# First loads in smaller parts, two fewer matmuls of ones, and the turned norms at another place in TensorE's order: a two-layer encoder trunk in fp32

## The chip, the cores and the metric

The kernel runs on one core of one Trainium2 chip. The metric is device time in microseconds (us) for one execution. The kernel before was run three times: median 651.51 us, lowest 651.26, highest 651.71.

## What is computed

The reference is a trunk of two layers over 512 tokens of width 1024. Layer 0 mixes tokens by neighbourhood attention, layer 1 by latent attention. After each layer a gated per-layer embedding is added. Only the start of the program matters for this change:

```python
xn = rmsnorm(x, norm_g[0])                      # x / sqrt(mean(x*x) + 1e-6) * g
q, k, v, z = split(xn @ w_in, 4)                # mixer_na
...
y = (o * silu(z)) @ w_out
h = x + y
gate = sigmoid(rmsnorm(h, ple_norm[0]) @ ple_w_gate[0])
x = h + gate * (p[0] @ ple_w_proj[0])
```

`p[0] @ ple_w_proj[0]` depends on no other result and can be computed first. `z` can be computed from x times its gains without the norm, and multiplied by each token's inverse norm afterwards.

## The kernel before

Every matrix product is done with fp32 values split in two parts: `hi` is a copy in the matmul's format, written by ScalarE, and `lo` is what is left, written by VectorE or GpSimd. A product of two split operands takes three matmuls: hi·hi, hi·lo and lo·hi. A matmul has 128 rows and 512 columns.

The start of `run` (from L1190) goes like this.

- `NWARM` = 11 matmuls of a constant of ones into a scratch PSUM tile open TensorE's work (L1192, L1193). Their result is not used.
- `ple_load` (L648) loads layer 0's p (`pT`) and its two weight tiles (`proj`), each 128x1024, in halves of 128x512 (256 KB). The halves of `pT` are issued by ScalarE's queue, the four of `proj` by SyncE's (L656). Each half is split by ScalarE (L658, `whi`) and VectorE (L659, `wlo`).
- SyncE then issues the gains, the eight tiles of x transposed (L1209), the weights of the first two z tiles in halves (L1216), the identity, and x with the third z tile's weights (L1224, L1225).
- `ple` computes p times the weights. Its first two output tiles, for tokens 0 to 127 and 128 to 255, are written in an order of their own (L677 to L679): for each of them first the three matmuls of the first half of the contraction, then those of the second half.
- `z_phase` with `ws` computes the first two z tiles (L201, 48 matmuls); without it the next three: z2 from weights already split, z3 and z4 from weights loaded by `load_w` (L99 the load, L100 `wwhi` on ScalarE, L101 `wwlo` on GpSimd).
- The inverse norms of the tokens (`ssq`) come from four sums of squares on ScalarE (L1226) and three short operations on GpSimd (L1228 to L1230). Four transposes of 128x128 on TensorE (L156, called by L1231) spread them over a PSUM tile, "the turns" below. ScalarE copies it to `R` (L1234). VectorE multiplies z0 and z1 by `R` (L193), and then x transposed by the turned tile and the gains (L1238); ScalarE and VectorE split that (L1239 `xh`, L1240 `xl`). The q and k products (L418) use it.

A tile scheduler sets the order of the instructions on each engine, except where `issue_after` or `InOrder` pins one behind another. Each engine works through its own instructions in that order. A DMA of SyncE or ScalarE is issued by a place in that engine's order. The buffers of `wraw`, `whi` and `wlo` are three each and are reused in turn.

Of the kernel before, what the change touches and what calls it, by code (L numbers as in the profile page):

```python
# [13 lines left out]
F32 = mybir.dt.float32  # L14
F32R = mybir.dt.float32r
AF = mybir.ActivationFunctionType
ALU = mybir.AluOpType
AX = mybir.AxisListType
PSUM = bass.MemoryType.PSUM
P = 128  # L20
S = 512
D = 1024
NT = S // P
KD = D // P
# [1 line left out]
EPS = 1e-6  # L26
NEG = -3.0e38
QSC = 96.0 ** -0.5
NWARM = 11
NLATE = 3  # L30
NEARLY = 7
SEVEN = (0, 1)
# [24 lines left out]
class Trunk:  # L57
# [123 lines left out]
    def z_phase(self, wap, xT, js, after=None, R=None, ws=None, first=None):  # L181


        zs = {}
        nc = self.nc

        def finish(j, ps):
            z = zs[j] = self.zp.tile([P, S], F32, name="z", tag="z")
            with self.tc.issue_after(after) if after is not None else nullcontext():
                if R is None:  # L190
                    nc.scalar.activation(z, ps, AF.Silu)
                else:
                    nc.vector.tensor_tensor(out=z, in0=ps, in1=R, op=ALU.mult)  # L193
                    nc.scalar.activation(z, z, AF.Silu)

        if ws:
            pss = [self.psum("mm") for j in js]
            for k in range(0, KD, 2):
                for ps, w in zip(pss, ws):
                    for i, (l, r) in enumerate(self.terms(w, xT, (k, k + 1))):  # L200
                        nc.tensor.matmul(ps, l, r, start=k == 0 and i == 0, stop=k == KD - 2 and i == 5)  # L201
            for j, ps in zip(js, pss):
                finish(j, ps)
            return zs
        for j in js:
            w = first if first and j == js[0] else self.load_w(wap[j], 1024)
            ps = self.psum("S" if R is not None and j < 4 else "mm")
            self.proj_T(ps, w, xT)
            finish(j, ps)
        return zs  # L210

# [433 lines left out]
    def ple_load(self, layer, pool=None):  # L645

        nc, a = self.nc, self.a
        if layer:  # L648
            return [self.load_w(ap, 1024) for ap in (a["pT"][1], a["proj"][1, 0], a["proj"][1, 1])]
        t = [[pool.tile([P, 1024], d, name=n, tag="p" + n, bufs=3) for n, d in (("wraw", F32), ("whi", F32R), ("wlo", F32R))]  # L650
             for _ in range(3)]
        src = (a["pT"][0], a["proj"][0, 0], a["proj"][0, 1])
        last = None
        for i, c0, c1 in [(i, c, c + S) for c in (0, S) for i in (1, 0)] + [(2, 0, S), (2, S, 2 * S)]:
            raw, hi, lo = (x[:, c0:c1] for x in t[i])
            (nc.sync if i else nc.scalar).dma_start(raw, src[i][:, c0:c1])  # L656
            with self.tc.issue_after(last.ins) if last else nullcontext():
                last = nc.scalar.activation(hi, raw, AF.Copy)  # L658
            nc.vector.tensor_tensor(out=lo, in0=raw, in1=hi.bitcast(F32), op=ALU.subtract)  # L659
        return [(hi, lo) for raw, hi, lo in t]  # L660

    def ple(self, pool, layer, tag, bufs, operands):
        nc, a = self.nc, self.a
        pT = operands[0]
        first = []
        for n in range(2):
            wj = operands[1 + n]
            for t in range(NT):
# [4 lines left out]
                if n == 0 and t < 2:  # L673
                    first.append((pp, m))
                    if t == 1:
                        last = None
                        for i in (0, 1, 2, 6, 7, 8, 3, 4, 5, 9, 10, 11):  # L677
                            with self.tc.issue_after(last.ins) if last else nullcontext():
                                last = nc.tensor.matmul(first[i // 6][0], *first[i // 6][1][i % 6], start=i % 6 == 0, stop=i % 6 == 5)  # L679
                else:  # L680
                    self.mms(pp, m)
                if n == 0 and t == 0:
# [494 lines left out]
    def run(self):  # L1177
        tc, nc, a = self.tc, self.nc, self.a
# [9 lines left out]
        with tc.tile_pool(name="pre", bufs=4, reuse_waits="tile") as pool:  # L1188
            R = pool.tile([P, S], F32, name="R", bufs=1)
            ones = [nc.const_aps.tensor(1.0, (P, n), mybir.dt.bfloat16) for n in (P, S)]  # L1190
            ps = self.psum("T")
# [3 lines left out]
            g0 = pool.tile([P, KD], F32, name="g0", bufs=1)  # L1195
            nc.sync.dma_start(g0, a["g0"])

            raw, xT = pair("r"), pair("x")
# [4 lines left out]
            xs = [xk[k // 4][:, k % 4, :] for k in range(KD)]  # L1203
# [24 lines left out]
            nc.gpsimd.tensor_scalar(ss, ss, 1.0 / D, EPS, op0=ALU.mult, op1=ALU.add)  # L1228
            nc.gpsimd.tensor_scalar(self.rows[0][0], ss, 1.0, None, op0=ALU.add)
            nc.gpsimd.tensor_tensor(out=ss, in0=ss, in1=self.half.to_broadcast([P, NT]), op=ALU.pow)  # L1230
            turned = self.transposes([ss[:, t:t + 1].to_broadcast([P, P]) for t in range(NT)])  # L1231
            nc.scalar.activation(first[1], first[0], AF.Copy)
            nc.gpsimd.tensor_tensor(out=first[2], in0=first[0], in1=first[1].bitcast(F32), op=ALU.subtract)
            nc.scalar.activation(R, turned, AF.Copy)  # L1234
            zs = self.z_phase(a["na_z"], raw, range(2), R=R, ws=ws)
            for k in range(KD):
                hi, lo = part(xT, k)
                nc.vector.scalar_tensor_tensor(xs[k], turned, g0[:, k:k + 1], xs[k], op0=ALU.mult, op1=ALU.mult)  # L1238
                nc.scalar.activation(hi, xs[k], AF.Copy)  # L1239
                nc.vector.tensor_tensor(out=lo, in0=xs[k], in1=hi.bitcast(F32), op=ALU.subtract)  # L1240
            zs.update(self.z_phase(a["na_z"], raw, range(2, 8 - NLATE), R=R, first=first[1:]))
# [239 lines left out]
```

## Time and profile before

| | |
|---|---|
| median of 3 runs | 651.51 us (651.26 to 651.71) |
| the profiled execution, its own time | 651.45 us |
| its span | 649.3 us (2.15 us lie around it) |
| TensorE busy | 639.7 us, 99% of the span |
| ScalarE, VectorE, GpSimd busy | 454.6, 429.6 and 407.3 us |

TensorE (PE in the rows) is busy nearly all the time, and the weight loads (PEld) run beside its matmuls. Three more views matter: which waits PE had, what stands at the start of the program in order of time, and what stands around the turns.

### The profile page before, as it was taken

What the parts mean: (1) busy time and instruction counts of PE and PEld (TensorE: products, weight loads), DVE (VectorE), ACT (ScalarE), POOL (GpSimd) and SP (SyncE); (2) the same over time, 40 slices, a digit from 0 to 9 for tenths busy, and PEclk for the clock granted to TensorE, in tenths of its full rate; (3) what the DMA queues carried; (4) which work ended last, traced back from release to release, by engine and by line L of the source; (5) the groups of instructions that cost most, each with busy time, mean ns of one, the idle gap of its engine ahead of it and who ended that gap; (6) DMA issues with size and microseconds to landing.
All of it is one profiled execution on the core that took longest, in us unless ns stands there. A gap on an engine that the chain in (4) does not pass through costs nothing.

```text
span 649.3 us, 9981 instructions
## 1 busy us (share of the span) xinstructions
PE 639.7 (99%) x3299; PEld 541.9 (83%) x3299; DVE 429.6 (66%) x887; ACT 454.6 (70%) x903; POOL 407.3 (63%) x370
## 2 busy tenths in 40 slices
PE   9999999999999999999999999999999999999994
PEld 6888888888888888888999888888888888888884
DVE  6197995665665626569715515888988885574665
ACT  7575776887887752797644536888989897547855
POOL 0371015777978673896655515786959887437974
PEclk9999999999999999999999999999999999999998
DMA  9939725878968988354642254120111222683514
GB/s 327 357 129 298 222 97 193 243 195 213 255 197 208 238 204 325 132 182 172 220 138 99 78 135 133 46 58 24 54 46 66 65 95 102 234 293 121 194 66 163
DMA packets 46131, 107.41 MB, mean 165 GB/s; under 512 B 4736, under 2 KB 17792, under 8 KB 46080
## 3 DMA queue, kind: packets, MB, share of 16 engines
q1 hardware_dynamic: 34608, 87.12, 39.1%
q0 software_dynamic: 11040, 18.88, 13.5%
q10 hardware_dynamic: 432, 0.79, 0.3%
q8 instruction: 26, 0.43, 0.3%
q14 instruction: 25, 0.20, 0.1%
HBM read 95.23 MB, written 25.17 MB: 185 GB/s over the span
## 4 chain that ended last, share of the span: by engine, by line
PE 98%; ACT 1%; DVE 0%; issue 0%; POOLq 0%; POOL 0%; DVEq 0%; ACTq 0%
PE ps_mm L124 28%; PE ps_S L124 12%; PE ps_mm L965 7%; PE ps_T L156 6%; PE ps_T L857 5%; PE ps_O L1077 5%; PE ps_mm L857 3%; PE ps_mm L418 3%; PE ps_T L302 3%; PE ps_S L857 3%; PE ps_T L124 3%; PE ps_O L124 2%; PE ps_O L613 2%; PE ps_mm L915 2%; PE ps_S L302 2%; PE ps_mm L201 2%
## 5 line engine op out<-in xcount | busy, mean ns | idle before, releaser
L101 POOL TENSOR_TENSOR wwlo<-wraw,wwhi 128x1024 fp32r<-128x1024 f32 (+5 forms) x68 | 121.1, 1795 | 96.5 <-ACT wwhi L100 45.6
L802 POOL TENSOR_TENSOR wlo<-wraw,whi 128x512 fp32r<-128x512 f32 x56 | 73.7, 1351 | 24.8 <-ACT whi L800 18.6
L1062 POOL TENSOR_TENSOR ex<-ex,rc 128x512 f32<-128x512 f32 x64 | 66.3, 1045 | 25.9 <-DVE rc L1061 22.0
L100 ACT ACTIVATE wwhi<-wraw 128x1024 fp32r<-128x1024 f32 (+5 forms) x71 | 55.1, 799 | 33.9 <-PE ps_mm L124 18.0
L1060 ACT ACTIVATE ex<-ps_S,mx 128x512 f32<-128x512 f32 x64 | 44.0, 687 | 11.8 <-DVE mx L1058 9.9
L587 POOL TENSOR_TENSOR ex<-ex,rc 128x128 f32<-128x128 f32 (+1 forms) x64 | 38.0, 699 | 18.2 <-DVE rc L583 18.1
L1058 DVE TENSOR_REDUCE mx<-ps_S 128x1 f32<-128x512 f32 x64 | 43.7, 683 | 8.3 <-PE ps_S L124 7.8
L113 DVE TENSOR_TENSOR pt_lo<-ps_T,pt_hi 128x512 fp32r<-128x512 f32 x64 | 43.2, 682 | 7.1 <-ACT pt_hi L111 6.7
L111 ACT ACTIVATE pt_hi<-ps_T 128x512 fp32r<-128x512 f32 x64 | 37.7, 594 | 3.4 <-PE ps_T L156 3.0
L156 PE MATMUL ps_T<-ident,ex 128*128 128x128 f32 x256 | 38.3, 272 | 0.0
L156 PEld LDWEIGHTS ps_T<-ident,ex 128*128 128x128 f32 x256 | 31.5, 140 | 7.5
L124 PE MATMUL ps_mm<-xh,wwhi 128*128 128x512 f32 x120 | 33.2, 401 | 0.0
L222 DVE TENSOR_TENSOR u<-ps_O,u 64x512 f32<-64x512 f32 x32 | 22.0, 686 | 16.7 <-ACT u L221 15.8
L800 ACT ACTIVATE whi<-wraw 128x1024 fp32r<-128x1024 f32 x28 | 29.2, 1054 | 5.0 <-PE ps_mm L124 2.8
L124 PE MATMUL ps_mm<-xl,wwhi 128*128 128x512 f32 x120 | 32.5, 399 | 0.0
L581 ACT ACTIVATE ex<-ex,mx 128x128 f32<-128x128 f32 (+1 forms) x64 | 30.2, 473 | 2.9 <-DVE mx L570 2.3
L124 PE MATMUL ps_mm<-xh,wwlo 128*128 128x512 f32 x120 | 31.1, 394 | 0.0
L124 PE MATMUL ps_S<-ko,qo 128*128 128x512 f32 x96 | 28.9, 409 | 0.0
L124 PE MATMUL ps_S<-ke,qe 96*128 96x512 f32 x96 | 28.6, 406 | 0.0
L965 PE MATMUL ps_mm<-cT,wwhi 128*128 128x512 f32 x94 | 27.7, 393 | 0.0
L226 POOL TENSOR_TENSOR u<-u,z 128x512 f32<-128x512 f32 x16 | 23.2, 1486 | 4.9 <-DVE u L222 4.8
L124 PEld LDWEIGHTS ps_mm<-xh,wwlo 128*128 128x128 f32 x120 | 22.0, 188 | 4.6
(489 smaller groups left out, 1912.8 us busy)
## 6 DMA issues: line engine op xcount, KB each, us to landing
sum<-gate POOLq DMA_DIRECT2D x12, 1024.0 KB, 8.9
wraw<-na_qk SPq DMA_DIRECT2D x16, 512.0 KB, 4.1
wraw<-sum SPq DMA_DIRECT2D x16, 512.0 KB, 3.2
pe<-pe SPq DMA_DIRECT2D x31, 256.0 KB, 6.5
wraw<-gate SPq DMA_DIRECT2D x12, 512.0 KB, 3.3
wraw<-na_v SPq DMA_DIRECT2D x10, 512.0 KB, 3.3
sum<-sum POOLq DMA_DIRECT2D x4, 1024.0 KB, 10.4
wraw<-na_o SPq DMA_DIRECT2D x8, 512.0 KB, 5.4
```

The source lines that it names most:

```text
L100: nc.scalar.activation(hi[:, c], raw[:, c], AF.Copy)
L101: f = lambda e, c=c: e.tensor_tensor(out=lo[:, c], in0=raw[:, c], in1=hi[:, c].bitcast(F32), op=ALU.subtract)
L113: self.dve.tensor_tensor(out=lo, in0=src, in1=hi.bitcast(F32), op=ALU.subtract)
L124: last = self.last_mm = nc.tensor.matmul(out, l, r, start=i == 0, stop=i == n - 1)
L156: self.last_mm = self.nc.tensor.transpose(t[:, i * P:(i + 1) * P], b, self.ident)
L587: self.last_norm = nc.gpsimd.tensor_tensor(out=e, in0=e, in1=rc[:, qt:qt + 1].to_broadcast([P, e.shape[1]]), op=ALU.mult)
L802: nc.gpsimd.tensor_tensor(out=lo[:, o], in0=raw[:, o], in1=hi[:, o].bitcast(F32), op=ALU.subtract)
L857: mm = nc.tensor.matmul(ps, l, r, start=j == 0 and p in banks, stop=j == 11 and p in (2, 3, 4), skip_group_check=True)
L965: self.last_mm = nc.tensor.matmul(PS[key], *terms[i], start=i == 0, stop=i == len(terms) - 1)
L1058: nc.vector.reduce_max(mx, sp, axis=AX.X, negate=True)
L1060: nc.scalar.activation(ex, sp, AF.Exp, bias=mx, accum_out=sm)
L1062: nc.gpsimd.tensor_tensor(out=ex, in0=ex, in1=rc.to_broadcast([P, S]), op=ALU.mult)
```

## The change

There are three parts. The first loads are cut differently: the first half of `proj`'s first tile and the first half of `pT` come as two parts of 128x256 (128 KB) each, `proj`'s on SyncE's queue and `pT`'s on ScalarE's. The second halves, still 256 KB, and the second weight tile all go to SyncE's queue. All of these loads are issued first, and the splits are pinned in the order of the pieces on ScalarE and on VectorE. The order of the first two tiles' matmuls takes lo·hi of p before hi·lo. `NWARM` goes from 11 to 9. The turns are pinned directly behind the last matmul of z0 and z1, and z2, z3 and z4 are pinned behind the turns' last.

```diff
-NWARM = 11
+NWARM = 9
...
-                        nc.tensor.matmul(ps, l, r, start=k == 0 and i == 0, stop=k == KD - 2 and i == 5)
+                        self.last_mm = nc.tensor.matmul(ps, l, r, start=k == 0 and i == 0, stop=k == KD - 2 and i == 5)
+            R = R()
...
-            self.proj_T(ps, w, xT)
+            with self.tc.issue_after(self.last_mm.ins) if R is not None else nullcontext():
+                self.proj_T(ps, w, xT)
...
-        last = None
-        for i, c0, c1 in [(i, c, c + S) for c in (0, S) for i in (1, 0)] + [(2, 0, S), (2, S, 2 * S)]:
+        act, dve, sp = (InOrder(self.tc, e) for e in (nc.scalar, nc.vector, nc.sync))
+        pieces = ((1, 0, 256, 0), (0, 0, 256, 1), (1, 256, S, 0), (0, 256, S, 1), (1, S, 2 * S, 0), (0, S, 2 * S, 0),
+                  (2, 0, S, 0), (2, S, 2 * S, 0))
+        for i, c0, c1, q in pieces:
+            (act if q else sp).dma_start(t[i][0][:, c0:c1], src[i][:, c0:c1])
+        for i, c0, c1, q in pieces:
             raw, hi, lo = (x[:, c0:c1] for x in t[i])
-            (nc.sync if i else nc.scalar).dma_start(raw, src[i][:, c0:c1])
-            with self.tc.issue_after(last.ins) if last else nullcontext():
-                last = nc.scalar.activation(hi, raw, AF.Copy)
-            nc.vector.tensor_tensor(out=lo, in0=raw, in1=hi.bitcast(F32), op=ALU.subtract)
+            act.activation(hi, raw, AF.Copy)
+            dve.tensor_tensor(out=lo, in0=raw, in1=hi.bitcast(F32), op=ALU.subtract)
...
-                        for i in (0, 1, 2, 6, 7, 8, 3, 4, 5, 9, 10, 11):
+                        for z, i in enumerate((0, 2, 1, 6, 7, 8, 3, 5, 4, 9, 11, 10)):
...
-            turned = self.transposes([ss[:, t:t + 1].to_broadcast([P, P]) for t in range(NT)])
...
-            nc.scalar.activation(R, turned, AF.Copy)
-            zs = self.z_phase(a["na_z"], raw, range(2), R=R, ws=ws)
+            turned = []
+
+            def turn():
+                with tc.issue_after(self.last_mm.ins):
+                    turned.append(self.transposes([ss[:, t:t + 1].to_broadcast([P, P]) for t in range(NT)]))
+                nc.scalar.activation(R, turned[0], AF.Copy)
+                return R
+
+            zs = self.z_phase(a["na_z"], raw, range(2), R=turn, ws=ws)
```

On SyncE's queue, at the program's start, before (`wraw` are the tiles as loaded, `g` the gains):

```order
L656 DMA wraw<-proj 128x512 x4
L1196 DMA g_152<-g 128x8
L1209 DMA xT<-xT 128x512 x4
L1216 DMA wraw<-na_z 128x512 x2
L1209 DMA xT<-xT 128x512 x4
```

and with the change:

```order
L51 DMA wraw<-proj 128x256 x2
L51 DMA wraw<-proj 128x512
L51 DMA wraw<-pT 128x512
L51 DMA wraw<-proj 128x512 x2
L1200 DMA g_156<-g 128x8
L1213 DMA xT<-xT 128x512 x4
```

The queue has two issues more ahead of the gains and of x. ScalarE's queue still has two, of half the size.

On TensorE, from the last matmuls of z0 and z1 to z3's `lo` weights, before (`ps_S_393` is z2, `ps_S_427` z3, `ps_mm_461` z4):

```order
L201 MATMUL ps_mm_314<-rh1_155,wlo_171 128x512 x2
L124 MATMUL ps_S_393<-rh0_154,whi_173 128x512 x4
L124 MATMUL ps_S_393<-rh1_155,whi_173 128x512 x4
L124 MATMUL ps_S_393<-rl0_156,whi_173 128x512 x4
L124 MATMUL ps_S_393<-rl1_157,whi_173 128x512 x4
L124 MATMUL ps_S_393<-rh0_154,wlo_174 128x512
L156 MATMUL ps_T_305<-ident_71,ssq_212 128x128 x4
L124 MATMUL ps_S_393<-rh0_154,wlo_174 128x512 x3
L124 MATMUL ps_S_393<-rh1_155,wlo_174 128x512 x4
L124 MATMUL ps_S_427<-rh0_154,wwhi_422 128x512 x4
```

and with the change (`ps_S_397` is z2, `ps_S_431` z3):

```order
L201 MATMUL ps_mm_312<-rh1_159,wlo_175 128x512 x2
L156 MATMUL ps_T_361<-ident_71,ssq_216 128x128 x4
L124 MATMUL ps_S_397<-rh0_158,whi_177 128x512 x4
L124 MATMUL ps_S_397<-rh1_159,whi_177 128x512 x4
L124 MATMUL ps_S_397<-rl0_160,whi_177 128x512 x4
L124 MATMUL ps_S_397<-rl1_161,whi_177 128x512 x4
L124 MATMUL ps_S_397<-rh0_158,wlo_178 128x512 x4
L124 MATMUL ps_S_397<-rh1_159,wlo_178 128x512 x4
L124 MATMUL ps_S_431<-rh0_158,wwhi_426 128x512 x4
```

The turns stand 17 matmuls earlier. Between them and z3's first matmul there are now 24 matmuls of z2, where there were 7.

On ScalarE, behind the last two sums of squares, before (`wwhi_422` is z3's weights, `wwhi_456` z4's):

```order
L1226 ACTIVATE x_163,ssq_212<-x_163 128x1024 x2
L100 ACTIVATE wwhi_422<-wraw_421 128x1024
L1234 ACTIVATE R_112<-ps_T_305 128x512
L100 ACTIVATE wwhi_456<-wraw_455 128x1024
L194 ACT_TABLE_LOAD
L194 ACTIVATE z_363<-z_363 128x512
```

and with the change (`wwhi_426` is z3's weights, `wwhi_460` z4's):

```order
L1230 ACTIVATE x_167,ssq_216<-x_167 128x1024 x2
L1242 ACTIVATE R_112<-ps_T_361 128x512
L194 ACT_TABLE_LOAD
L194 ACTIVATE z_367<-z_367 128x512
L194 ACTIVATE z_370<-z_370 128x512
L1249 ACTIVATE xh0_162<-xT_168 128x512 x2
L100 ACTIVATE wwhi_426<-wraw_425 128x1024
L1249 ACTIVATE xh0_162<-xT_168 128x512 x2
L1249 ACTIVATE xh1_163<-xT_169 128x512
L100 ACTIVATE wwhi_460<-wraw_459 128x1024
```

The split of z3's weights stood ahead of R; it now stands behind R, the load of the SiLU table, two SiLUs and two copies of the scaled x.

## Rows read from the trace of the kernel before

**Rows 1.** The page: busy time by engine, and the chain that ended last by engine.

```profile
PE 639.7 (99%) x3299; PEld 541.9 (83%) x3299; DVE 429.6 (66%) x887; ACT 454.6 (70%) x903; POOL 407.3 (63%) x370
...
PE 98%; ACT 1%; DVE 0%; issue 0%; POOLq 0%; POOL 0%; DVEq 0%; ACTq 0%
```

**Rows 2.** Waits of the weight loads, whole span: total us, times, longest.

```profile
PEld ps_mm L679 <- ACT whi L658: 0.5, 1, 0.5
PEld ps_S L124 <- DVE mx L573: 0.4, 1, 0.4
PEld ps_mm L679 <- DVE wlo L659: 0.3, 1, 0.3
```

**Rows 3.** Timeline of PE, 0 to 7.2 us: start us, us, engine, line, what.

```profile
0.76 4.85 PE L1193 MATMUL ps_T<-const-bfloat16-1.0 128*128 128x512 bf16 x11 [0.76 <-PEq L1470]
5.25 0.79 PE L679 MATMUL ps_mm<-whi 128*128 128x512 f32 x1
5.84 0.53 PE L679 MATMUL ps_mm<-wlo,whi 128*128 128x512 f32 x1
6.21 0.39 PE L679 MATMUL ps_mm<-whi,wlo 128*128 128x512 f32 x1
...
6.67 0.40 PE L679 MATMUL ps_mm<-wlo,whi 128*128 128x512 f32 x1
```

**Rows 4.** Timeline of ACT and DVE, 0 to 9 us: the first splits.

```profile
1.64 1.28 ACT L658 ACT_TABLE_LOAD   x1 [1.64 <-PEq L1470]
4.05 1.15 ACT L658 ACTIVATE whi<-wraw 128x512 fp32r<-128x512 f32 x2 [1.13 <-DMA wraw<-proj]
...
4.71 1.29 DVE L659 TENSOR_TENSOR wlo<-wraw,whi 128x512 fp32r<-128x512 f32 x2 [3.86 <-ACT whi L658]
```

**Rows 5.** DMA issues at 0.7 us: queue, count, size, us from issue to landing.

```profile
wraw<-proj SPq DMA_DIRECT2D x1, 256.0 KB, 3.3
```

**Rows 6.** DMA issues at 1.17 us.

```profile
wraw<-proj SPq DMA_DIRECT2D x1, 256.0 KB, 4.6
```

**Rows 7.** DMA issues of 485 to 496 us, with nothing else on the DMA engines.

```profile
wraw<-proj SPq DMA_DIRECT2D x4, 256.0 KB, 2.9
```

**Rows 8.** Timeline of ACT at 640 us: an operation of 256 columns.

```profile
640.63 0.45 ACT L809 ACTIVATE ps_O<-ps_O,rs 128x256 f32<-128x256 f32 x1
```

**Rows 9.** Timeline of PE, 26.9 to 34 us: around the turns.

```profile
27.11 0.61 PE L201 MATMUL ps_mm<-rh,wlo 128*128 128x512 f32 x2
...
29.37 1.98 PE L124 MATMUL ps_S<-rl,whi 128*128 128x512 f32 x8
...
31.41 0.60 PE L156 MATMUL ps_T<-ident,ssq 128*128 128x128 f32 x4
31.77 1.87 PE L124 MATMUL ps_S<-rh,wlo 128*128 128x512 f32 x7
33.47 0.84 PE L124 MATMUL ps_S<-rh,wwhi 128*128 128x512 f32 x3
```

**Rows 10.** Timeline of ACT, 26 to 46 us.

```profile
30.24 1.06 ACT L100 ACTIVATE wwhi<-wraw 128x1024 fp32r<-128x1024 f32 x1 [6.71 <-DMA wraw<-na_z]
32.05 0.60 ACT L1234 ACTIVATE R<-ps_T 128x512 f32<-128x512 f32 x1 [0.74 <-PE ps_T L156]
...
33.61 1.28 ACT L194 ACT_TABLE_LOAD   x1
...
36.91 2.18 ACT L1239 ACTIVATE xh<-xT 128x512 fp32r<-128x512 f32 x4
```

**Rows 11.** Timeline of DVE, 30 to 50 us.

```profile
33.88 5.35 DVE L1238 SCALAR_TENSOR_TENSOR xT<-ps_T,g,xT 128x512 f32<-128x512 f32 x8
```

**Rows 12.** Timeline of POOL, 23 to 27 and 31 to 47 us.

```profile
24.23 1.04 POOL L1230 TENSOR_TENSOR ssq<-ssq,half 128x4 f32<-128x4 f32 x1
...
36.57 2.41 POOL L101 TENSOR_TENSOR wwlo<-wraw,wwhi 128x1024 fp32r<-128x1024 f32 x1 [0.40 <-ACT wwhi L100]
...
41.93 4.37 POOL L101 TENSOR_TENSOR wwlo<-wraw,wwhi 128x1024 fp32r<-128x1024 f32 x1 [2.95 <-PE ps_S L124]
```

More of the change, by code (lines that the diff above doesn't have):

```diff
@@ L676, in ple @@
                         last = None
-                        for i in (0, 1, 2, 6, 7, 8, 3, 4, 5, 9, 10, 11):
+                        for z, i in enumerate((0, 2, 1, 6, 7, 8, 3, 5, 4, 9, 11, 10)):
                             with self.tc.issue_after(last.ins) if last else nullcontext():
-                                last = nc.tensor.matmul(first[i // 6][0], *first[i // 6][1][i % 6], start=i % 6 == 0, stop=i % 6 == 5)
+                                last = nc.tensor.matmul(first[i // 6][0], *first[i // 6][1][i % 6], start=i % 6 == 0, stop=z in (8, 11))
                 else:
@@ L1230, in run @@
             nc.gpsimd.tensor_tensor(out=ss, in0=ss, in1=self.half.to_broadcast([P, NT]), op=ALU.pow)
-            turned = self.transposes([ss[:, t:t + 1].to_broadcast([P, P]) for t in range(NT)])
             nc.scalar.activation(first[1], first[0], AF.Copy)
             nc.gpsimd.tensor_tensor(out=first[2], in0=first[0], in1=first[1].bitcast(F32), op=ALU.subtract)
-            nc.scalar.activation(R, turned, AF.Copy)
-            zs = self.z_phase(a["na_z"], raw, range(2), R=R, ws=ws)
+            turned = []
[5 more added lines that the diff above has]
+            zs = self.z_phase(a["na_z"], raw, range(2), R=turn, ws=ws)
             for k in range(KD):
                 hi, lo = part(xT, k)
-                nc.vector.scalar_tensor_tensor(xs[k], turned, g0[:, k:k + 1], xs[k], op0=ALU.mult, op1=ALU.mult)
+                nc.vector.scalar_tensor_tensor(xs[k], turned[0], g0[:, k:k + 1], xs[k], op0=ALU.mult, op1=ALU.mult)
                 nc.scalar.activation(hi, xs[k], AF.Copy)
```

## The prediction

> **What bounds the kernel now.** I read the page first. TensorE is busy 99% of the span and holds 98% of the chain that ended last [rows 1], so time is to be had only on TensorE: fewer matmuls, or fewer pauses between them. Second, the waits of its weight loads [rows 2]: over 649 us there are three, together 1.2 us. Two of them are at the very start (0.5 us for the first `whi`, 0.3 us for a `wlo`), the third (0.4 us) lies in the attention heads, which this change does not touch. Third, therefore, the timeline of the start [rows 3]. From the third product at 6.21 us on, TensorE runs from matmul to matmul. A step that starts its stream of products sooner moves the whole program by as much, as long as nothing later makes it wait. A step on another engine is worth nothing by itself and can only cost.
>
> What stands ahead of that stream: eleven matmuls of ones from 0.76 us. They take 4.85 us with the last one's 0.63, so one starts every (4.85 - 0.63) / 10 = 0.42 us, which is 512 columns at 1.2 GHz, the lower level of the clock. The first product is shown from 5.25 us. The second, at 5.84, takes 0.53, between the 0.63 of a slow matmul and the 0.39 of a fast one. So the clock rises to 2.4 GHz while it runs, near 6.1 us. The third starts at 6.21, the fifth at 6.67; from there one starts every 0.227 us ((1.98 - 0.39) / 7 in [rows 9]).
>
> What the first product waits for [rows 4]: ScalarE has its table by 2.92, then waits 1.13 us for the first part of `proj` until 4.05, and splits that and the first part of `pT` in 1.15 us, until 5.20. The load was issued at about 0.72 and took 3.3 us [rows 5].
>
> **The first loads and the nine matmuls.** These go together, since the later of the two sets the start.
>
> The matmuls of ones: two fewer at 0.42 us free TensorE 0.85 us sooner. A tenth slot would begin at 0.76 + 9 x 0.42 = 4.56 us.
>
> The data: the first product now needs two parts of `proj` and one of `pT`, 384 KB instead of 512. 256 KB took 3.3 us with as much beside it [rows 5] and 2.9 alone [rows 7]. The first 128 KB, with 128 KB beside it, should then land by 0.72 + 2.9 = 3.6 us, and is of no use before the table's end at 2.92. I take 3.3, since half the bytes are to be moved until then. The second part of `proj` lies between 2.92 and 4.6, by when all 512 KB had landed before, since ScalarE split both halves without a pause [rows 4]; I take 4.1, since the same 512 KB are on the way until then. ScalarE needs at most 0.45 us for 256 columns [rows 8] in place of 0.6. The two first pieces are then done by 4.2, the second of `proj` by 4.55. That meets the end of the ninth matmul of ones: first product at about 4.56.
>
> The following operands: the `lo` of `pT` is ready before 4.6 and that of `proj` by 5.0, since the order of the second and third product was swapped for it. So the 0.3 us wait for a `wlo` [rows 2] goes. The seventh product needs the second half of `proj`, which landed at 5.77 before [rows 6] and is split by about 6.4 even if it comes no sooner. That product is due at 6.63, so it does not wait; the cover is 0.2 us.
>
> The clock: I assume that it rises at 6.1 us again, since TensorE is busy from 0.76 us on in both. The products then start at 4.56, 4.98, 5.40 and 5.83. By 6.1 two thirds of the fourth are through, the rest takes 0.08, and the fifth starts at 6.18. Before, it started at 6.67. **Gain: 0.48 us**, not the 0.85 of two matmuls nor the 1.2 of slots and wait together, because products that come sooner run at the lower level. Had the rise moved forward with the products (0.7 us after the first, which came to run at 5.41 before), the fifth would start at 5.8 and the gain be 0.9; the row alone doesn't exclude that, and I keep it inside the forecast's range. The Trainium skill ("TensorE: Matmul & The Clock Gate", Part 1) calls the warm-up a budget of time and not of a number of matmuls. By that rule the sum stays at 0.48; one execution before can't show it.
>
> The two added issues on SyncE's queue: each takes 0.45 us, so x and the weights behind them are issued up to 0.9 us later. That has cover. TensorE needs the sums of squares at the turns only: `ssq` is ready at 24.23 + 1.04 = 25.27 [rows 12], the turns come at 27.56 - 0.48 = 27.1 [rows 9], 1.8 us later. I cost it at nothing. If that cover went, each us beyond it would be a us of TensorE. The two more operations on ScalarE and VectorE in the split fall into times when both wait for loads.
>
> **The turns.** TensorE does the same four transposes. They cost 0.47 us of its stream: from 31.41 to 33.47 less seven matmuls of 0.227 [rows 9]. That is paid before and after alike, so nothing comes of the move itself.
>
> But the move changes what ScalarE does in between, and there the change adds a wait. I count from the first turn. R starts 0.64 us after it and ends at 1.24 (32.05 against 31.41, 0.60) [rows 9, 10]. The table load takes 1.28, until 2.54. Two SiLUs and two copies of 512 columns follow, one every 0.52 us ((2.18 - 0.62) / 3 in [rows 10]), until about 4.64. Only then comes the split of z3's weights, 1.06 us: done at 5.7. VectorE is no hindrance: its scaled x begins at 33.88 - 31.41 = 2.47 and comes every 0.67 us [rows 11], so the second is there by 3.9. TensorE reaches z3 after the turns and 24 matmuls, 0.47 + 24 x 0.227 = 5.9 us, and its weight load comes 0.22 before that, at 5.7. Before, that split was done at 31.3, two us ahead of its use at 33.47 [rows 9, 10]. So what had two us of cover now has none. If the operations follow each other without overlap, the split ends at 6.1 and TensorE waits 0.4 us; if they overlap as in the rows, 0 to 0.1. Below nothing is excluded: TensorE does not come sooner for it. **Cost: 0.1 us**, since the nearest rows are of these very operations.
>
> Behind it on ScalarE stand z4's and the q and k weights. GpSimd gets z3's at 5.7 after the turn, needs 2.4 us [rows 12], and TensorE wants them 16 matmuls after z3's first, at 9.3: 1.2 us to spare. One row of the same operation took 4.37 us beside VectorE's splits [rows 12]; here those begin at 7.8 and can touch only its end. z4's weights have over 2 us. Freed later, those buffers delay the next loads, of the v weights, by up to 2 us; TensorE is 15 us from using them.
>
> **Sum.** 0.48 - 0.1 = 0.4 us less. The profiled execution took 651.45, which is 0.06 under the median of 651.51; against that median I predict 651.1 us. A measurement of this kernel can tell about 0.2% (1.3 us) from no change, so this is "the same".
>
> **Rivals.**
>
> *The rise does not bind.* If the clock rises before 4.56 us, the fifth product starts at 4.56 + 4 x 0.227 = 5.47 and the gain is 1.2 us, 1.1 with the cost at z3: 650.4. Against it: the row has the rise near 6.1. For it: that is one execution, and three of the kernel differ by 0.45 us, as much as one or two products at either level. The same part of the Trainium skill says that the moment of the rise differs from run to run. Chance 0.17.
>
> *The parts land no sooner.* If the first 128 KB take the 3.3 us of the 256 KB, ScalarE starts at 4.05 again and three pieces of 0.35 to 0.45 end by 5.2. TensorE pauses 0.6 us, the gain is the swapped order's alone, some 0.2 us: 651.4. For it: the load takes 2.9 us even alone, most of it perhaps not for bytes. Chance 0.12.
>
> *z3 waits longer.* ScalarE's chain behind the turns holds a VectorE result and a hand-over in each step. At 0.5 us of wait the gain is gone; at 1 us the result is 652.0, slower than before. Against it: the rows of the same operations leave 0.4 at most. Chance 0.12.
>
> *The pause restarts the ramp.* Before, the matmuls of ones reached into the first product without a gap. If the parts land late, TensorE stands still between 4.6 and 5.2, and the clock may need as long again as it took before, 5.3 us from 0.76 to 6.1. From 4.6 on it would rise at 9.9. With the first product at 5.2 and one every 0.42, eleven would be through by then, where 18 were before (the fifth at 6.67, then one every 0.227). Seven products are 1.6 us lost: 653.1 with z3's cost. It decides from the point where the second part of `proj` is split later than 4.6. Against it: the gap would be short. Chance 0.09.
>
> **How the numbers follow.** My forecast has the remaining 0.50, with times of 650.7 to 651.4. The range 650.3 to 652.0 reaches to the fast rival on one side and z3's wait on the other, and leaves out the ramp and half a tenth at either edge. Faster by over 0.2% (under 650.2) needs the fast rival and no cost at z3, with other luck: 0.07. Slower by over 0.2% (over 652.8) needs the ramp or a wait of nearly 2 us at z3: 0.06. The same: 0.87.
>
> **What would show it.** In the profile after: nine matmuls of ones, then the first product near 4.6; the first ScalarE split near 3.3 rather than 4.05; the fifth product near 6.2; no wait for a `wlo` at the start; the four turns directly behind the last matmul of z1, near 27.1; z3's first matmul at 33.0 to 33.1, and perhaps a new wait of its weight load for `wwhi`; from there everything 0.3 to 0.5 us sooner. It is wrong if the fifth product is not earlier, if the turns wait for `ssq`, or if a wait over 0.5 us stands at z3 or further on.

## The result, and the profile after

The change made the kernel slower, by little: 652.63 us median (652.31 to 653.66, 13 runs) against 651.55 (651.26 to 651.91, 13 runs) for the kernel before on the same chip. The ratio is 1.0019, 95% interval 1.0011 to 1.0027, so about 1.1 us more. The prediction was 651.1, with a range up to 652.0. The profiled execution took 652.71, of which the span is 650.9; before it was 651.45 and 649.3.

The page of the kernel after, busy time and the chain by engine, as [rows 1]:

```profile
PE 640.1 (98%) x3297; PEld 541.7 (83%) x3297; DVE 434.0 (67%) x889; ACT 455.1 (70%) x905; POOL 407.1 (63%) x370
...
PE 92%; DVE 4%; ACT 1%; issue 1%; POOLq 0%; POOL 0%; DVEq 0%; ACTq 0%
```

TensorE's own work is the same within 0.4 us. But the chain now runs over VectorE for 4% of the span, where it had 0%, and VectorE is busy 4.4 us longer, with only two short instructions more. The waits of the weight loads (total us, times, longest), as [rows 2], say where that is felt:

```profile
PEld ps_S L304 <- ACT s L51: 1.7, 2, 1.5
PEld ps_mm L683 <- ACT whi L51: 1.1, 2, 0.7
PEld ps_S L124 <- ACT whi L51: 0.4, 1, 0.4
PEld ps_S L124 <- DVE mx L575: 0.4, 1, 0.4
```

The wait of 1.5 us is new; the prediction had named a wait over 0.5 us further on as a sign of being wrong. L304 is the products for v, `s` is ScalarE's copy of the PSUM tile that the first of them leaves and the second goes on with, and L51 is the helper that records operations pinned in order. The two `whi` rows lie at the start.

**The start.** Timeline of PE, as [rows 3]:

```profile
4.52 0.80 PE L683 MATMUL ps_mm<-whi 128*128 128x512 f32 x1
...
6.24 0.40 PE L683 MATMUL ps_mm<-wlo,whi 128*128 128x512 f32 x1
6.47 0.40 PE L683 MATMUL ps_mm<-whi,wlo 128*128 128x512 f32 x1
6.87 0.50 PE L683 MATMUL ps_mm<-whi 128*128 128x512 f32 x1
7.21 0.40 PE L683 MATMUL ps_mm<-whi,wlo 128*128 128x512 f32 x1
7.53 0.50 PE L124 MATMUL ps_S<-whi 128*128 128x512 f32 x1
...
9.47 0.84 PE L124 MATMUL ps_T<-whi 128*128 128x512 f32 x3
```

The first product starts at 4.52 and the fifth at 6.24, 0.43 us sooner than in [rows 3]. Then the seventh waits for the second half of `proj`, and the ninth, which belongs to the third token tile, for the second half of `pT`. The seventeenth, the first on `ps_T`, starts at 9.47; before it was 9.43. In this execution the gain was there, and was all but given back by the ninth product. ScalarE, as [rows 4], waits 1.42 us for the second group of loads:

```profile
3.36 1.41 ACT L51 ACTIVATE whi<-wraw 128x256 fp32r<-128x256 f32 x4 [0.43 <-DMA wraw<-proj]
6.19 2.73 ACT L51 ACTIVATE whi<-wraw 128x512 fp32r<-128x512 f32 x4 [1.42 <-DMA wraw<-proj]
```

The DMA engines were full all that time. The window from 2 to 6 us, in the view by windows (the last three numbers are the granted clock as a share of full speed, the DMA engines' busy share, and GB/s), of the kernel before:

```profile
2.00:6.00 4.00, 4.00 (x11) 1.55 (x9) 1.29 (x2) 2.31 (x4) 0.00 (x0) 1.00 1.00 331
```

and of the kernel after:

```profile
2.00:6.00 4.00, 4.00 (x11) 1.93 (x10) 1.45 (x4) 2.34 (x5) 0.00 (x0) 1.00 0.97 285
```

Busy alike, they moved 285 GB/s instead of 331. In four us that is 184 KB less, which fits with a later landing of what stands third in the queue. The clock reads 1.00 in both rows, although the matmuls of ones start one every 0.42 us there, which is the lower level; at the start of the program the clock is told by the matmuls and not by this number.

**Around the turns.** Timeline of PE, as [rows 9]:

```profile
27.61 0.60 PE L156 MATMUL ps_T<-ident,ssq 128*128 128x128 f32 x4
...
33.52 2.00 PE L124 MATMUL ps_S<-rh,wwhi 128*128 128x512 f32 x8
```

The turns stand directly behind z1, without a wait, and z3 starts at 33.52, where it started at 33.47. Up to here nothing is lost or won. Then ScalarE, as [rows 10]:

```profile
32.25 1.05 ACT L100 ACTIVATE wwhi<-wraw 128x1024 fp32r<-128x1024 f32 x1
...
47.84 0.63 ACT L194 ACTIVATE z<-z 128x512 f32<-128x512 f32 x1 [6.44 <-DVE z L193]
48.38 1.04 ACT L51 ACTIVATE whi<-wraw 128x1024 fp32r<-128x1024 f32 x1
...
61.37 0.60 ACT L51 ACTIVATE s<-ps_S 128x512 f32<-128x512 f32 x1
```

It sat 6.44 us idle until VectorE's multiply for z3, and the first split of the v weights, at 48.38, stands behind that. Before, that split stood ahead of z3's SiLU, and the copy `s` still had to wait for TensorE. ScalarE before:

```profile
42.79 1.06 ACT L51 ACTIVATE whi<-wraw 128x1024 fp32r<-128x1024 f32 x1
...
59.51 0.60 ACT L51 ACTIVATE s<-ps_S 128x512 f32<-128x512 f32 x1 [0.26 <-PE ps_S L302]
```

VectorE, as [rows 11], with the change:

```profile
35.35 3.83 DVE L1250 TENSOR_TENSOR xl<-xT,xh 128x512 fp32r<-128x512 f32 x2
39.10 0.68 DVE L193 TENSOR_TENSOR z<-ps_S,R 128x512 f32<-128x512 f32 x1
39.70 7.50 DVE L1250 TENSOR_TENSOR xl<-xT,xh 128x512 fp32r<-128x512 f32 x6
47.13 0.68 DVE L193 TENSOR_TENSOR z<-ps_S,R 128x512 f32<-128x512 f32 x1
```

Eight lower splits of the scaled x took 11.3 us. In the kernel before, seven of them took 4.30, 0.6 each:

```profile
39.75 4.30 DVE L1240 TENSOR_TENSOR xl<-xT,xh 128x512 fp32r<-128x512 f32 x7
```

And GpSimd, as [rows 12], had four operations in one row at that time, where before it paused between the third and the fourth:

```profile
33.38 10.87 POOL L101 TENSOR_TENSOR wwlo<-wraw,wwhi 128x1024 fp32r<-128x1024 f32 x4 [5.35 <-ACT wwhi L100]
```

The end of it on TensorE:

```profile
60.30 0.61 PE L304 MATMUL ps_S<-wlo,xh 128*128 128x512 f32 x2
62.02 0.72 PE L304 MATMUL ps_S<-whi,xh 128*128 128x512 f32 x2 [1.11 <-ACT s L51]
```

Pairs there follow each other at 0.45 us, so this one was due at 60.75: 1.27 us lost. The q and k products behind it start at 67.68; before it was 66.11. Of these 1.57 us, 0.08 were there ahead of the v products, and the other 0.2 were lost in the pairs behind the wait.

### The profile page after: what moved, and what is told of

Read it like the earlier page. It is cut to its first block, busy times and chain, and to the rows that moved or that the text cites. A ratio compares the mean times of both kernels' runs of the same rounds, so it can differ in the third digit from the quotient of the medians.

```text
span 650.9 us, 9987 instructions
## 1 busy us (share of the span) xinstructions
PE 640.1 (98%) x3297; PEld 541.7 (83%) x3297; DVE 434.0 (67%) x889; ACT 455.1 (70%) x905; POOL 407.1 (63%) x370
## 4 chain that ended last, share of the span: by engine, by line
PE 92%; DVE 4%; ACT 1%; issue 1%; POOLq 0%; POOL 0%; DVEq 0%; ACTq 0%
PE ps_mm L124 27%; PE ps_S L124 11%; PE ps_mm L969 7%; PE ps_T L156 6%; PE ps_T L861 5%; PE ps_O L1081 5%; PE ps_mm L861 3%; PE ps_T L304 3%; PE ps_S L861 3%; PE ps_T L124 3%; PE ps_O L124 2%; PE ps_O L615 2%; PE ps_mm L919 2%; DVE xl L1250 2%; PE ps_mm L420 2%; PE ps_mm L201 2%
```

## The experiments

Theory A: the move of the turns makes VectorE's splits and GpSimd's operations for the q and k weights run at the same time, each slows the other, and z3's multiply, the v weights and the second v product follow late. Its rival: the first loads are to blame, by their two issues more or their later landing. The kernel before was run beside each, with medians of 651.4 to 651.5.

**The two parts apart.** `turns_only` keeps the first loads and eleven ones of before; `loads_only` has the new loads and nine ones, and the turns where they were.

```diff
 turns_only
-NWARM = 9
+NWARM = 11
...
-        pieces = ((1, 0, 256, 0), (0, 0, 256, 1), (1, 256, S, 0), (0, 256, S, 1), (1, S, 2 * S, 0), (0, S, 2 * S, 0),
...
+        for i, c0, c1 in [(i, c, c + S) for c in (0, S) for i in (1, 0)] + [(2, 0, S), (2, S, 2 * S)]:
...
 loads_only, against the kernel before
-NWARM = 11
+NWARM = 9
...
-        for i, c0, c1 in [(i, c, c + S) for c in (0, S) for i in (1, 0)] + [(2, 0, S), (2, S, 2 * S)]:
...
+        pieces = ((1, 0, 256, 0), (0, 0, 256, 1), (1, 256, S, 0), (0, 256, S, 1), (1, S, 2 * S, 0), (0, S, 2 * S, 0),
...
```

> The turns behind z0 and z1, with the loads, their order and the eleven matmuls of ones as before. Theory A (the move of the turns costs the time: VectorE's splits of the scaled x now run beside GpSimd's four weight splits, z3's multiply stands behind the last of them, ScalarE's first v split behind z3's SiLU, and so the copy of the first v product comes too late for TensorE): the wait of the second v product for that copy is there, 1.2 to 1.7 us, and the time is 652.7 to 653.2. Theory B (the later loads push the sums of squares and with them everything behind R; the move alone is harmless): no such wait, 651.3 to 651.7.

> The loads in parts, their order and the nine matmuls of ones, with the turns where the scheduler had put them before. Theory A: the products start 0.4 to 0.5 us sooner and lose that again by the tenth, since the third load lands later than before; from there as before, no wait at the v products: 651.3 to 651.8. Theory B: the wait at the v products is there without the move of the turns: 652.3 to 652.9.

The turns alone: 653.06 us (652.80 to 653.56), ratio 1.0025 [1.0015, 1.0035]. The loads alone: 651.69 (651.36 to 652.78), ratio 1.0005 [0.9996, 1.0013]. So the loss comes with the move of the turns. The waits of the weight loads with the turns alone hold the same row:

```profile
PEld ps_S L304 <- ACT s L51: 1.7, 2, 1.5
```

The loads alone wait only 0.4 us in total at v. Their start shows both halves of the story:

```profile
4.60 0.50 PE L681 MATMUL ps_mm<-whi 128*128 128x512 f32 x1
4.93 0.40 PE L681 MATMUL ps_mm<-whi,wlo 128*128 128x512 f32 x1
...
8.03 0.50 PE L124 MATMUL ps_S<-whi 128*128 128x512 f32 x1 [0.87 <-ACT whi L51]
...
9.98 0.84 PE L124 MATMUL ps_T<-whi 128*128 128x512 f32 x3
```

In this execution the clock was at 2.4 GHz from the first product on, which is the condition of the prediction's rival of 650.4. It brought nothing: the ninth product waited 0.87 us, the seventeenth started at 9.98, later than before, and the execution took 652.13.

**Take the wait's links away, one at a time.** `z3_first` is the whole change with z3's multiply pinned ahead of the last four lower splits. `no_qk_rest` is the whole change, where GpSimd writes zeros instead of computing the lower parts of the first q and k weights (its output lacks those terms).

```diff
 z3_first
...
+            for k in range(4, KD):
+                hi, lo = part(xT, k)
+                with tc.issue_after(self.last_times.ins):
+                    nc.vector.tensor_tensor(out=lo, in0=xs[k], in1=hi.bitcast(F32), op=ALU.subtract)
 no_qk_rest
+            if empty:
+                nc.gpsimd.memset(lo[:, c].bitcast(F32), 0.0)
+                continue
...
-            weights = {0: [self.load_w(a["na_qk"][i], 1024) for i in (0, 8)]}
+            weights = {0: [self.load_w(a["na_qk"][i], 1024, empty=True) for i in (0, 8)]}
```

> The whole change, with z3's multiply by R put ahead of VectorE's last four splits of the scaled x and nothing else in any engine's order changed. Theory A in the form that the place of this multiply is what holds ScalarE: ScalarE starts its first v split at 43 to 44 instead of 48.4 us, the chain behind it is about 2 us sooner, the wait of TensorE is gone or under 0.3 us: 651.2 to 651.7. In the form that the splits themselves are what is late, whatever stands between them: the wait stays over 1 us, 652.3 to 652.8.

> The whole change, but the lower parts of the first q and k weights are not computed: GpSimd clears them instead, 1 us each in place of 2.4 to 3. Theory A with contention between VectorE and GpSimd: the six later splits of the scaled x take 0.6 to 0.7 us each in place of 1.25, z3's multiply comes near 43.5 in place of 47.1 us, and TensorE's wait at the v products is under 0.3 us: 651.2 to 651.7. Without contention (the splits are slow for a reason of their own): they stay at 1.2 us each and the time at 652.3 to 652.9.

`z3_first`: 651.71 (651.17 to 652.21), ratio 1.0004 [0.9995, 1.0013]. z3's multiply starts at 44.88, the wait at v is down to 0.4 us, and with it the loss. `no_qk_rest`: 651.23 (650.71 to 652.09), ratio 0.9998 [0.9989, 1.0007], and no wait at v. Its VectorE:

```profile
35.41 3.82 DVE L1253 TENSOR_TENSOR xl<-xT,xh 128x512 fp32r<-128x512 f32 x2
39.16 0.68 DVE L196 TENSOR_TENSOR z<-ps_S,R 128x512 f32<-128x512 f32 x1
39.76 3.69 DVE L1253 TENSOR_TENSOR xl<-xT,xh 128x512 fp32r<-128x512 f32 x6
```

The same six splits take 3.69 us, not 7.50, once GpSimd reads nothing beside them, and the copy `s` again waits for TensorE, by 2.04 us. The two that still run beside GpSimd's operations for z3 and z4 take 3.82, as in the change. The kernel also frees GpSimd and the buffers of the weights sooner (its clears took 0.93 us each), so its time alone is no price of the contention; the rows are.

**The same with all of the work done.** `lo_late` pins GpSimd's two operations behind VectorE's last split; `lo_wait` makes GpSimd read one column of that split first. `turns_lo` is `turns_only` with the same.

```diff
 lo_late
+                last_xl = nc.vector.tensor_tensor(out=lo, in0=xs[k], in1=hi.bitcast(F32), op=ALU.subtract)
...
+            weights = {0: [self.load_w(a["na_qk"][i], 1024, behind=last_xl.ins) for i in (0, 8)]}
 lo_wait, turns_lo
+            seen = nc.gpsimd.tensor_scalar(ss[:, :1], xT[1][1][:, 3, :1].bitcast(F32), 1.0, None, op0=ALU.mult)
+            weights = {0: [self.load_w(a["na_qk"][i], 1024, behind=seen.ins) for i in (0, 8)]}
```

> The whole change, with one wait more: GpSimd's two lower parts of the first q and k weights are pinned behind VectorE's last lower split of the scaled x. The order on every engine is that of the change. Theory A (VectorE is slowed by GpSimd's work at the same time, and so the v weights come late): the last six splits take 3.7 to 4.5 us instead of 7.5, z3's multiply starts at 43.4 to 44.2 instead of 47.1, the second v product does not wait over 0.5 us, and the time is 651.1 to 651.5 with all of the computation in it. Rival: the buffers of the q and k weights come free later, so the next weights are loaded later and the wait at the v products comes back in another form, time 652 to 653.

> The whole change, all of its computation, and one operation more on GpSimd: between the lower parts of z4's weights and those of the first q weights it multiplies one element a row of the last lower split of the scaled x into a scratch column, so that it waits until VectorE has written it. (The run before only pinned an order, which on different engines gave no wait: GpSimd's four operations stood at 33.10 to 43.96 again.) Theory A (VectorE is slowed by GpSimd's work at the same time): GpSimd's two operations for q and k start at 43 to 44, the last six splits take 3.7 to 4.5 us instead of 7.5, z3's multiply starts at 43.3 to 44.3 instead of 47.1, the second v product does not wait over 0.5 us, and the time is 651.1 to 651.6. Rival: the time is 652.4 or more, since the two buffers come free 4 to 5 us later, the second and third v weights are loaded later, and the v products wait for those.

> The turns moved, the first loads and eleven ones as before, and the same waiting operation on GpSimd. Theory A: against the 653.06 of the turns alone the wait at the second v product goes and the time is 651.3 to 651.7, no different from the kernel before, since the move itself is worth nothing. If the move of the turns has another cost, the time stays over 652.3.

`lo_late` missed: the pin orders instructions of one engine and made GpSimd wait for nothing. Its four operations stood at 33.10 to 43.96 again, so this is the change once more: 652.99, ratio 1.0022 [1.0014, 1.0031], the same wait of 1.5 us.

`lo_wait` took 656.73 (656.60 to 658.60), ratio 1.0088, `turns_lo` 656.85, ratio 1.0083. The six splits came as theory A has them, but so did the rival, and it decides the time. VectorE of `lo_wait`:

```profile
39.76 3.69 DVE L1250 TENSOR_TENSOR xl<-xT,xh 128x512 fp32r<-128x512 f32 x6
43.37 0.68 DVE L193 TENSOR_TENSOR z<-ps_S,R 128x512 f32<-128x512 f32 x1
```

But GpSimd's two operations now run beside VectorE's first two subtractions for the v weights, which take 3.86 us instead of 1.29: the contention is moved, not removed. And the q and k buffers come free 5 us later, so the third split of v weights waits for its load. ScalarE, and what TensorE does of it, both of `lo_wait`:

```profile
57.83 1.06 ACT L51 ACTIVATE whi<-wraw 128x1024 fp32r<-128x1024 f32 x1 [5.09 <-DMA wraw<-na_v]
...
64.64 0.73 PE L304 MATMUL ps_S<-whi,xh 128*128 128x512 f32 x2 [3.68 <-ACT s L51]
```

That pair was due at 60.81, so 3.8 us are lost, three times what the change loses there. The move of the turns by itself therefore stays without a clean price; in `z3_first`, with z3's multiply pinned and all of the work done, the whole change costs nothing that can be told.

**The first loads.** Four kernels ask what the start could give. `nine_only` is the kernel before with nine ones. `act3` is `loads_only` with the second half of `pT` issued by ScalarE's queue. `z3_act3` is `z3_first` with the same. `pool_part` is `loads_only` with the second part of `proj` issued by GpSimd's queue.

```diff
 nine_only
-NWARM = 11
+NWARM = 9
 act3, z3_act3
-        pieces = (..., (1, S, 2 * S, 0), (0, S, 2 * S, 0),
+        pieces = (..., (1, S, 2 * S, 0), (0, S, 2 * S, 1),
 pool_part
-        pieces = ((1, 0, 256, 0), (0, 0, 256, 1), (1, 256, S, 0), ...
+        pieces = ((1, 0, 256, 0), (0, 0, 256, 1), (1, 256, S, 2), ...
...
-            (act if q else sp).dma_start(t[i][0][:, c0:c1], src[i][:, c0:c1])
+            (sp, act, nc.gpsimd)[q].dma_start(t[i][0][:, c0:c1], src[i][:, c0:c1])
```

> The kernel before with nine matmuls of ones in place of eleven, its loads in halves as before. The scheduler also puts z3's multiply behind the last split of the scaled x on VectorE here, but leaves ScalarE's first v split ahead of z3's SiLU. If the matmuls of ones only fill the wait for the first load: first product at 5.25 as before, no loss unless the clock rises later, 651.3 to 651.8. If the pause of 0.6 us makes the clock rise later: its rise over 8 us, 652.5 to 653.1. If the place of z3's multiply on VectorE alone is enough for the wait at the v products: 652.7 to 653.2; if ScalarE's order is needed for it too, no such wait.

> The loads in parts without the move of the turns, with the second half of p issued by ScalarE's queue as its third, ahead of its table load, instead of by SyncE's fourth. Theory A (a first load lands a fixed time after its issue, so those that the parts push back by one or two issues land 0.45 or 0.9 us later, and that eats what the start gains): the half of p lands near 6.4 in place of 6.8, the wait ahead of the ninth product shrinks by 0.3 to 0.5 us, the first product comes no later than 4.7, and the time is 651.1 to 651.5. Rival (the loads share one bandwidth, whatever their order of issue): the landings stay within 0.1 us and the time within 651.5 to 651.9.

> The whole change with z3's multiply ahead of VectorE's last four splits and the second half of p on ScalarE's queue. If the two repairs add up: 651.2 to 651.6, no wait over 0.4 us at the v products, the ninth product sooner than 7.5. If the v products' chain (VectorE and GpSimd side by side) sets the pace from 40 us on whatever the start gains: the wait at the v products grows by what the start gained and the time stays at 651.6 to 651.9.

> The loads in parts without the move of the turns, with the second part of the weights issued by GpSimd's queue, so that the second half of the weights and the second half of p move up by one issue each on SyncE's. Theory A: the half of the weights lands near 5.7 in place of 6.1, the seventh product starts near 6.4, the ninth near 7.0, 0.5 us sooner than before the change: 650.9 to 651.3. Rival (GpSimd's queue delivers later than SyncE's by over 0.5 us): the first product starts after 5 us and nothing is gained: 651.4 to 651.9.

`nine_only`: 653.22, ratio 1.0032 [1.0019, 1.0044]. Its start:

```profile
5.29 0.50 PE L679 MATMUL ps_mm<-whi 128*128 128x512 f32 x1 [0.83 <-ACT whi L658]
...
6.67 0.40 PE L679 MATMUL ps_mm<-wlo,whi 128*128 128x512 f32 x1
```

The fifth product starts at 6.67, to the hundredth as in [rows 3]: the two ones do not matter, and a pause of 0.83 us did not lower the clock. It is slower for waits further on:

```profile
PEld ps_S L302 <- ACT s L51: 1.0, 2, 0.8
PEld ps_S L124 <- ACT wwhi L100: 0.7, 1, 0.7
PEld ps_mm L418 <- DVE xl L1240: 0.6, 2, 0.4
```

The last two lie ahead of the first v product, which starts at 56.24 instead of 55.23: the scheduler put the split of z3's weights behind R here too. The first is the wait of the change at v. For that one the scheduler had put z3's multiply behind all eight lower splits (8.57 us), but ScalarE's first split of the v weights stood ahead of z3's SiLU, at 43.70. So the place of the multiply on VectorE is enough for this wait, without ScalarE's order and without the move of the turns. Why the scheduler orders it so in these kernels is not known.

`act3` (652.38, ratio 1.0017 [1.0008, 1.0025]) and `z3_act3` (652.62, ratio 1.0018 [1.0009, 1.0027]) missed. ScalarE of `act3`:

```profile
7.43 1.68 ACT L51 ACTIVATE whi<-wraw 128x512 fp32r<-128x512 f32 x3 [2.52 <-DMA wraw<-proj]
```

The second half of `proj`, issued at the same place as in the change, was there at 7.43 and not at 6.19. The DMA engines were 95% busy from 2 to 6 us; that the half of `pT` on the other queue took its share of them is a reading and was not tried by itself.

`pool_part` missed too: 654.92, ratio 1.0061 [1.0047, 1.0074]. GpSimd's part took 5.4 us from issue to landing, where 2.9 were seen on SyncE's queue, and the first product came at 7.11:

```profile
7.11 0.78 PE L681 MATMUL ps_mm<-whi 128*128 128x512 f32 x1 [2.78 <-ACT whi L51]
7.68 0.63 PE L681 MATMUL ps_mm<-whi,wlo 128*128 128x512 f32 x1
```

**Rows instead of columns.** If the parts carry less because their rows are 1 KB, halves of rows of 2 KB should not. `rows_cut` is `loads_only`, `rows_lo` is `lo_late`, with each first half cut into 64 rows on SyncE's and 64 on ScalarE's queue; the order of the first twelve products follows the pieces.

```diff
+            for e, r in ((sp, slice(0, P // 2)), (act, slice(P // 2, P))) if n < 2 else ((sp, slice(0, P)),):
+                e.dma_start(t[i][0][r, c0:c1], src[i][r, c0:c1])
```

> First loads and nine ones as in the change, turns as before, but the first halves are cut by rows: proj's first half as 64x512 on SyncE's and 64x512 on ScalarE's queue, pT's the same, rows of 2 KB instead of 1 KB; everything behind them on SyncE. Theory L (bytes): from 2 us on the DMA engines are fully busy (share 0.9 to 1.1 in each us), and with the 256-column parts they move less: 1140 KB in the four us from 2 to 6, against 1326 KB before; that is why the third load lands later. Then with 2 KB rows the sum from 2 to 6 us is back at 1300 KB or more, proj's second half lands by 5.7, no product from the seventh to the twelfth waits over 0.2 us, the seventeenth matmul of the stream (the first on the tile ps_T) starts at 8.9 to 9.1 (before 9.43, loads alone 9.98), and the time is about 651.1. Theory M (the landing is set by the place in the queue and a fixed time): 256 KB in third place lands at 6.1 as in the change, the seventh to ninth product wait 0.5 to 0.9 us again, the seventeenth matmul starts at 9.4 to 10, and the time is 651.6.

> Both edits together, on the whole change: first halves cut by rows, and the two lower parts pinned behind the last split. If theories A and L both hold, the seventeenth matmul starts at 8.9 to 9.1, no wait over 0.5 us stands at the v products, q and k begin at 65.7 to 65.9 (before 66.1), and the time is 650.9, that is 0.6 us under the kernel before. If only A holds: 651.3. If only L holds: 652.2.

`rows_cut` took 656.09 (ratio 1.0075), `rows_lo` 655.40 (1.0065): misses. `rows_cut` in the window from 2 to 6 us:

```profile
2.00:6.00 4.00, 2.77 (x7) 0.75 (x5) 0.00 (x0) 1.91 (x2) 0.00 (x0) 1.00 0.69 208
```

Only 208 GB/s, at a busy share of 0.69. The Trainium skill ("SBUF — State Buffer", Door 1: The DMA port swizzle, and Can I just issue two DMAs to hit both halves?) says that a transfer to 64 partitions reaches half of the ports and that two of them at once do not make up for it. The row of `rows_cut` would agree, but `rows_lo`, with the same loads, moved 277 GB/s at a share of 0.87, so the price of the halves is not settled here. ScalarE's table load also stood behind its two issues and a load, at 4.08 instead of 1.64, and the first product came at 7.98 and 6.53. So these runs do not decide between the theories of the loads.

What the traces hold on that: from 2 to 6 us the four executions with the first loads of before, in rows of 2 KB, moved 308 to 341 GB/s (before, `turns_only`, `nine_only`, `turns_lo`), the six with those of the change 276 to 292 (after, `loads_only`, `z3_first`, `no_qk_rest`, `lo_wait`, `lo_late`), all at a busy share of 0.94 to 1.03. That the row length is the cause, and not the order of the issues, was not tried by itself.

## Why the prediction was wrong

**The first loads, up to the fifth product: right.** First split at 3.36 (forecast 3.3), first product at 4.52 (4.56), fifth at 6.24 (6.18), gain 0.43 us (0.48). No wait for a `wlo` of these products. That the number fits is in part luck: the clock rose near 6.1 in this execution, as assumed, but by 5.8 or sooner in the other five with these loads, in three of them ahead of the first product.

**The cover of 0.2 us behind them: wrong.** The step that failed reads that the second half of `proj` "is split by about 6.4 even if it comes no sooner". That allowed for a landing as late as before, and none later. But its issue moved one place down the queue, and the engines moved 14% less. It landed near 6.1 where 5.77 had been read [rows 6], ScalarE began with it at 6.19, and the seventh product, due at 6.70, started at 6.87. The second half of `pT` went from ScalarE's queue to SyncE's fourth place, and the ninth product waited for it. The prediction had no line for that load at all. Together they took the 0.43 us back. Other executions differ, but on the whole nothing is left: the seventeenth product starts at 9.19 to 9.98 us in the six with the change's first loads, and at 9.28 to 9.65 in the four with those of before. `nine_only` and `loads_only` show that neither the ones nor the clock set this start, but the loads: the first two in `nine_only`, the third and fourth in `loads_only`.

**The turns: right, and z3's wait right.** No wait for `ssq`, the turns at 27.61, half a us later than forecast, by what the start had given back. ScalarE's chain came as counted: z3's split ended at 33.30, 5.69 after the first turn (forecast 5.7), and z3 started within 0.1 us of its slot.

**What stands behind it: wrong, and this decided.** The failed step is the last paragraph on the turns: GpSimd's work beside VectorE's splits "can touch only its end", and later loads of the v weights cost nothing because "TensorE is 15 us from using them". Three things in it failed.

- GpSimd had four operations to do, not one. ScalarE split the q and k weights right behind those of z3 and z4, so GpSimd ran from 33.38 to 44.25 without a pause. Before, it paused from 38.98 to 41.93, and half of the time of VectorE's seven splits fell into that pause; in the other half it was GpSimd's fourth operation that waited (4.37 us in [rows 12]).
- The price was put on GpSimd, whose operations went from 2.41 us to 2.7. VectorE paid: its splits went from 0.62 us to 2.2 on the mean of the four that ran while GpSimd was at work. Eight splits would take 5.0 us and took 11.3. `no_qk_rest` and `lo_wait` show the cause: the same six take 3.69 as soon as GpSimd reads nothing.
- The 15 us were not slack. From the split of the v weights at 48.38 to the second v product at 62.02 there are 13.6 us of work on ScalarE and VectorE that follow each other: splits, subtractions, the transform of x, the copy `s`. Before, that copy waited 0.26 us for TensorE, so no slack was to be had beyond that. And the v weights were late not for their load. VectorE's first subtraction for them started at 49.46 instead of 47.37. One half of these 2.1 us is VectorE's own: it was through with z3's and z4's multiplies 1.0 us later. In the other half it stood idle for 1.05 us, since the split of the weights stood behind z3's SiLU on ScalarE, which waited for z3's multiply at 47.13. In `z3_first`, without the second half, the subtraction starts at 48.48 and 0.4 us of wait is left; in `nine_only`, where VectorE alone is late (49.65), TensorE waits 1.0 us.

The sum was thus −0.4 where this trace has 0.1 for the start and z3 and about 1.5 for v; the medians differ by 1.1. Of the rivals, "z3 waits longer" had the sign and nearly the size (652.0), but the wrong place: z3 did not wait. "The rise does not bind" came true in single executions, and was worth nothing. "The pause restarts the ramp" fell for a pause about as short as feared: `nine_only` paused 0.83 us and ran on at 2.4 GHz. Longer ones did cost the clock (below).

## What to carry over

When a step moves on one engine, list everything that becomes ready behind it on the engines that it feeds, and lay the streams of VectorE and GpSimd over each other in time: a stretch that was quick only because the other engine paused or had to wait is a resource in use. Look, too, at where the scheduler then puts each result that another engine waits for. A distance to the next use on TensorE is cover only after the chain of other engines in between is taken off it. And with the DMA engines full, a first load that comes sooner is paid by the third and the fourth, so follow the start as far as the last load that was reordered.

## What was not expected of the hardware

- VectorE's subtraction of two 128x512 fp32 tiles took 0.62 us alone and up to 2.9 us beside GpSimd's subtraction of 128x1024, and GpSimd's went from 2.41 to 2.7. In [rows 12] it was GpSimd's turn to lose: 4.37 us. Why the one loses in one kernel and the other in the other is not shown. VectorE's multiply of the scaled x, which reads one operand from PSUM, was not slowed: 5.35 us for eight, beside GpSimd's subtractions in [rows 11] and [rows 12]. The Trainium skill ("SBUF — State Buffer", SBUF: two separate sides) describes a shared port pair that whichever engine starts first holds for its whole instruction. The trace of the change agrees with that: beside GpSimd's four operations four splits got through, and each ended 0.54 to 0.56 us after one of them had ended (at 35.82, 38.63, 41.46 and 44.25), which is a split that waits and not one at half speed.
- The moment of the clock's rise differed from execution to execution, with the same first matmul at 0.76 us: near 6.1 in the kernel before and after, ahead of 4.6 in `loads_only`, near 3.4 in `rows_lo`. The Trainium skill ("TensorE: Matmul & The Clock Gate", Part 1) says that it varies from run to run, by half a us either way. The traces agree that it varies, but over 2.7 us, and the measurement decides.
- A long wait can cost twice. After the 3.7 us in `lo_wait`, TensorE ran at half its clock. The windows from 65 us, in the view by windows (the number ahead of the last two is the granted clock):

```profile
65.00:66.00 1.00, 1.00 (x4) 0.78 (x3) 0.66 (x2) 1.00 (x3) 0.00 (x0) 0.63 1.03 270
66.00:67.00 1.00, 1.00 (x4) 0.80 (x3) 1.00 (x3) 0.96 (x2) 0.00 (x0) 0.50 1.04 270
67.00:68.00 1.00, 1.00 (x4) 0.81 (x3) 1.00 (x1) 0.00 (x0) 0.00 (x0) 0.50 1.06 254
68.00:69.00 1.00, 1.00 (x4) 0.77 (x4) 0.97 (x1) 0.97 (x2) 0.00 (x0) 0.66 1.06 209
```

The share of 0.50 is 1.2 GHz, from about 65.3 to 68.7 us, which costs another 1.7 us. The same was seen behind pauses of 2.37 us in `rows_lo` and 2.78 us in `pool_part`. Pauses of 0.83, 1.72 and 1.86 us (`nine_only`, `act3`, `z3_act3`) were followed by matmuls at 2.4 GHz.
